# Half of the low parts of x from GpSimd at the change of token halves, and two query columns' attention one step later

## The chip, the cores and the metric

The kernel runs on one core of a Trainium2 chip. The metric is the device time of one execution in microseconds (us); lower is better. The time before is the median of 3 runs.

## The reference, cut to what matters

The reference is one decoder layer: 2048 tokens of width D = 2048 through a normalisation, a sliding-window attention with 32 query heads and 4 key and value heads of 64, a gate, and an output product.

```python
h = rms_norm(x, swa_norm)
q, k, v, gate = split(h @ w_in, [2048, 2048 + 256, 2048 + 512])
q, k = rms_norm(q per head, q_gain), rms_norm(k per head, k_gain)
# blocks of 128 queries against their own and the previous block of keys
s = einsum(q, k) * 64 ** -0.5 + rel_table[t5_bucket(dist)]
s = where(in_band & not before the start, s, -inf)
m = maximum(max(s), sink)
p = exp(s - m); p = p / (sum(p) + exp(sink - m))
o = einsum(p, v)
out = x + (o * silu(gate)) @ w_out
```

All of it is float32. The kernel reaches that on TensorE by splitting each operand into a high and a low part (`h` and `l`) and adding three products: high by high, high by low, low by high.

## The kernel before, in words

**The projections.** The first part of the program has 40 steps. A step is one `gemm` (L147, L150, L153): 128 output columns of q, k or v for 1024 tokens, which is half of the sequence. Its 96 matmuls of 128x512 (16 chunks `k` of D, three products, two token quarters) fill two PSUM banks `acc`, called first and second bank here. Steps 0 to 19 make the first half of the tokens (k, v, eight q columns, k, v, eight q columns), steps 20 to 39 the second half in the same order. Four `acc` buffers serve them, so a step's banks are those of the step two before it, and can start once those have been read out. The weights come as 128x1024 tiles, are split by ACT (`wh`, L132) and POOL (`wl`, L133), with three buffers for each.

**The tokens.** `load_big(c)` brings in x transposed for one half: 16 tiles of 128x1024 through four `raw` buffers; ACT writes the high part scaled by the norm's gain (`bigh`, L100), DVE the low part (`bigl`, L101). For the second half this runs while TensorE works on the last steps of the first half. It is put ahead in priority, once step 19's gemm has been issued.

**The attention.** A `unit` is 256 queries of one query column (two heads): 128 units in all, four per column and half. `beside(n)` issues a step's units from the table `units`. A unit has 8 score matmuls `s` (L328), then on DVE a mask copy, four `lg` (L341), `mx` (L345), `nm` (L347) and `es` (L350), on ACT four exponentials (L354), on DVE `den`, on POOL `lg` times `den` (L359), then 4 transposes `pt` on TensorE (L363), `ph` by ACT (L365), `pl` by DVE (L367), four selects by POOL (L371, L373: `php`, `ph`, `plp`, `pl`), 8 matmuls `o` (L382), `bot` by ACT (L385), two `og` by DVE (L388). The PSUM pools for `s`, `pt` and `o`, and the tiles `ph`, `pl`, `php`, `plp`, have one buffer each, so units follow one another through them hand to hand.

**The hand-over of queries.** `evac_q` reads a q step's two banks: for each bank ACT writes `qq` (L212, in two pieces of 64 rows) and DVE its low part (L213), ACT the squares `sq` (L216). `qq` has four buffers, which is two steps, so the second bank of a step can be read only when the score matmuls that use the buffer from two query steps before have been done; the second bank of the step two later waits for that in its turn. `evac_k` and `evac_v` transpose a k or v step's result on TensorE, normalise and write it out (`kl`, L277).

**The order.** Each engine's instruction order is fixed when the program is built, by a scheduler which follows the program's order and priorities and its own idea of times. So a changed table of units gives another order of TensorE's work, also in places far from the change. Score matmuls of later units, `pt` and `o` of earlier ones, and the projection matmuls of one or two steps stand mixed in TensorE's row. After the 40 steps come gates and the output product (L497 and on), which the change does not touch.

Of the kernel before, what the change touches and what calls it, by code (L numbers as in the profile page):

```python
# [9 lines left out]
F32 = mybir.dt.float32  # L10
F32R = mybir.dt.float32r
I8 = mybir.dt.int8
AF = mybir.ActivationFunctionType
ALU = mybir.AluOpType
# [5 lines left out]
KT = D // P  # L20
HALF = 1024
NB = HALF // P
# [9 lines left out]
def swa_layer_kernel(ctx: ExitStack, tc: tile.TileContext, xT: bass.AP, x: bass.AP, w_in: bass.AP,  # L32
# [13 lines left out]
    nc = tc.nc  # L46
# [36 lines left out]
    gT = const.tile([P, KT], F32, name="gT")  # L83
# [8 lines left out]
    def load_big(c, ks=range(KT), cuts=(0, HALF), xsq=None):  # L92
        hi, lo = [], []
        for k in ks:
            raw = st.tile([P, HALF], F32, tag="raw", name="raw", bufs=RAW)
            h = big.tile([P, HALF], F32R, tag="big", name="bigh")
            l = big.tile([P, HALF], F32R, tag="big", name="bigl")
            for a, b in zip(cuts, cuts[1:]):
                nc.sync.dma_start(out=raw[:, a:b], in_=xT[k * P:(k + 1) * P, c * HALF + a:c * HALF + b])
                nc.scalar.activation(out=h[:, a:b], in_=raw[:, a:b], func=AF.Copy, scale=gT[:, k:k + 1])  # L100
                nc.vector.scalar_tensor_tensor(out=l[:, a:b], in0=raw[:, a:b], scalar=gT[:, k:k + 1],  # L101
                                               in1=h[:, a:b].bitcast(F32), op0=ALU.mult, op1=ALU.subtract)
                if xsq:
                    square_sums(k, raw, a, b, xsq)
            hi.append(h)
            lo.append(l)
        return hi, lo
# [50 lines left out]
    def square_sums(k, raw, a, b, xsq):  # L158

        for i in range(a, b, CH):  # L160
            cs = slice(i, i + CH)
            if k == 0:
                nc.scalar.activation(out=xsq[i // CH], in_=raw[:, cs], func=AF.Square)
            else:
                sq = evp.tile([P, CH], F32, tag="ev", name="xq")
                nc.scalar.activation(out=sq, in_=raw[:, cs], func=AF.Square)
                nc.gpsimd.tensor_tensor(out=xsq[i // CH], in0=xsq[i // CH], in1=sq, op=ALU.add)
# [235 lines left out]
    units = {}  # L403
    for n, (kind, c, i) in enumerate(steps):
        if kind == "q":
            for b in range(0, NB, 2):
                units.setdefault(n + 1 + b // 4, []).append((i, c * NB + b))

    def evacuate(step, acc, copies=None):
        kind, c, i = step  # L410
# [27 lines left out]
    def load_x(k):  # L438
        if k == 0:
            nc.sync.dma_start(out=gT, in_=g_norm)  # L440
        h, l = load_big(0, [k], (0, HALF) if k else (0, CH, HALF), xsq)
        res[0].extend(h)
        res[1].extend(l)
# [25 lines left out]
    for n, step in enumerate(steps):  # L469
        if n < 2:  # L470
            continue
        nxt = load_stat(stat_src(steps[n + 1]), eng=nc.gpsimd) if n + 1 < len(steps) else None
        if 4 <= n < 4 + NB:
            block_sums(NB + n - 4)
        elif n == 4 + NB:
            stats(1)
        beside(n)
        acc = gemm(stat, res)
        if n + 1 < len(steps) and steps[n + 1][1] != step[1]:
            with tc.high_priority(offset=300):  # L480
                res = load_big(1)
        evacuate(step, acc)
        stat = nxt
# [161 lines left out]
    for p, i in tiles:  # L645
# [12 lines left out]
        raw = a  # L658
# [70 lines left out]
```

## Time and profile before

| | us |
|---|---|
| median of 3 runs | 2556.72 (2553.59, 2556.72, 2557.89) |
| the profiled execution, its own time | 2552.12 |
| its span in the profile | 2550.4 |
| TensorE busy | 2467.7 (97%) |
| VectorE busy | 1651.6 (65%) |
| ScalarE busy | 973.7 (38%) |
| GpSimd busy | 1033.5 (41%) |

The granted clock of TensorE over the span was 0.986 of full speed. The busy times are sums over the span; an engine that is busy for two thirds of the whole can be the one that is waited for in a stretch of 30 us. "PE" is TensorE, "DVE" VectorE, "ACT" ScalarE, "POOL" GpSimd. A row of a timeline gives the start of an instruction, its duration, and in brackets the idle time in front of it with the operation that ended the idle time.

### The profile page before, as it was taken

To read this page: it belongs to the slowest core of one execution; us is meant where nothing else is said; L and a number is where in the kernel's file an instruction comes from. 1 tells how busy PE (TensorE), PEld (TensorE's weight loads), DVE (VectorE), ACT (ScalarE), POOL (GpSimd) and SP (SyncE) were. 2 spreads that over 40 slices of the span, in tenths; PEclk is the share of its full clock that TensorE was granted. 3 is DMA by queue.
4 is the path that set the end of the run, shared out by engine and by line. 5 is a ranking of instruction groups with operands and counts; after the bars stand their busy time and mean duration, and the time that the engine had idled before them with its cause. 6 is when DMAs were issued, how large, how long until landed. Compare 5 with 4: busy or idle time off the path is not lost.

```text
span 2550.4 us, 35219 instructions
## 1 busy us (share of the span) xinstructions
PE 2467.7 (97%) x11858; PEld 2048.9 (80%) x11858; DVE 1651.6 (65%) x3220; ACT 973.7 (38%) x2387; POOL 1033.5 (41%) x1011
## 2 busy tenths in 40 slices
PE   7999999999999999999999999999999999998898
PEld 5888888887888888888877887877787877787677
DVE  7387876789788785778737865676764345552432
ACT  6265654456555554455532331332223121121100
POOL 8366665666666675566512300122220220022122
PEclk9999999999999999999999999999999999999999
DMA  5433342125321214122259986887878586676653
GB/s 194 128 106 96 100 130 81 53 83 177 112 73 53 91 57 131 57 70 64 85 195 305 345 290 229 260 279 242 272 255 270 190 286 218 232 261 201 220 176 132
DMA packets 210228, 433.58 MB, mean 170 GB/s; under 512 B 20080, under 2 KB 91392, under 8 KB 210048
## 3 DMA queue, kind: packets, MB, share of 16 engines
q1 hardware_dynamic: 210048, 431.34, 52.2%
q8 instruction: 94, 1.54, 0.2%
q14 instruction: 86, 0.70, 0.1%
HBM read 341.07 MB, written 90.19 MB: 169 GB/s over the span
## 4 chain that ended last, share of the span: by engine, by line
PE 61%; DMA 19%; DVE 10%; issue 6%; POOL 2%; ACT 2%; SPq 1%; DVEq 0%; POOLq 0%; ACTq 0%
PE acc L147 17%; PE acc L153 17%; PE acc L150 17%; PE o L382 4%; PE s L328 4%; DMA braw<-w_out 3%; DMA braw<-xT 3%; DMA araw<-w_in 3%; DMA araw<-o_sp 3%; DMA out<-craw 2%; PE pt L363 2%; DMA araw<-s_sp 2%; DVE araw L497 1%; DVE wl L133 1%; DMA t_sp<-braw 1%
## 5 line engine op out<-in xcount | busy, mean ns | idle before, releaser
L147 PE MATMUL acc<-obh,wh 128*128 128x512 f32 x1536 | 495.8, 398 | 43.2 <-DVE craw L497 20.7
L147 PE MATMUL acc<-bigh,wh 128*128 128x512 f32 x1536 | 506.4, 398 | 15.9 <-ACT bigh L100 8.8
L150 PE MATMUL acc<-bigl,wh 128*128 128x512 f32 x1536 | 500.2, 397 | 3.7 <-DVE bigl L101 3.6
L153 PE MATMUL acc<-bigh,wl 128*128 128x512 f32 x1536 | 497.1, 395 | 1.8 <-DVE wl L133 1.8
L153 PE MATMUL acc<-obh,wl 128*128 128x512 f32 x1536 | 484.3, 394 | 3.6 <-DVE wl L133 3.6
L150 PE MATMUL acc<-obl,wh 128*128 128x512 f32 x1536 | 484.2, 394 | 0.0
L147 PEld LDWEIGHTS acc<-obh,wh 128*128 128x128 f32 x1536 | 293.0, 191 | 123.9 <-issue 19.0
L147 PEld LDWEIGHTS acc<-bigh,wh 128*128 128x128 f32 x1536 | 287.1, 190 | 75.5 <-ACT bigh L100 10.5
L153 PEld LDWEIGHTS acc<-obh,wl 128*128 128x128 f32 x1536 | 291.7, 190 | 67.3 <-DVE wl L133 5.7
L150 PEld LDWEIGHTS acc<-obl,wh 128*128 128x128 f32 x1536 | 292.8, 191 | 60.6
L150 PEld LDWEIGHTS acc<-bigl,wh 128*128 128x128 f32 x1536 | 285.7, 190 | 58.7 <-DVE bigl L101 7.8
L153 PEld LDWEIGHTS acc<-bigh,wl 128*128 128x128 f32 x1536 | 286.3, 189 | 56.6 <-DVE wl L133 2.6
L132 ACT CAST wh<-araw 128x512 fp32r<-128x512 f32 x224 | 137.2, 618 | 454.1 <-PE acc L150 387.9
L500 POOL TENSOR_TENSOR craw<-craw,u 128x512 f32<-128x512 f32 x64 | 89.3, 1406 | 464.4 <-DMA craw<-x 296.0
L354 ACT ACTIVATE lg<-lg,nm 128x128 f32<-128x128 f32 x512 | 199.9, 392 | 193.3 <-DVE nm L347 185.0
L500 POOL TENSOR_TENSOR craw<-craw,th 128x512 f32<-128x512 f32 x64 | 99.0, 1565 | 424.7 <-DVE th L613 353.1
L133 POOL TENSOR_TENSOR wl<-raw,wh 128x512 fp32r<-128x512 f32 x148 | 194.1, 1312 | 107.3 <-ACT wh L132 95.9
L497 DVE TENSOR_TENSOR araw<-araw 128x1024 f32<-128x1024 f32 x64 | 80.9, 1265 | 235.5 <-DMA araw<-o_sp 89.7
L133 DVE TENSOR_TENSOR wl<-araw,wh 128x512 fp32r<-128x512 f32 x224 | 182.3, 821 | 54.4 <-ACT wh L132 49.2
L540 ACT CAST obh<-braw 128x1024 fp32r<-128x1024 f32 x80 | 84.1, 1052 | 256.8 <-DVE braw L497 101.3
L359 POOL TENSOR_TENSOR lg<-lg,den 128x512 f32<-128x512 f32 x128 | 135.9, 1062 | 108.2 <-DVE den L358 68.4
L341 DVE SCALAR_TENSOR_TENSOR lg<-s,rq,bias 128x128 f32<-128x128 f32 x512 | 144.9, 343 | 38.1 <-PE pt L363 22.9
(115 smaller groups left out, 3491.7 us busy)
## 6 DMA issues: line engine op xcount, KB each, us to landing
araw<-w_in SPq DMA_DIRECT2D x88, 512.0 KB, 5.8
braw<-w_out SPq DMA_DIRECT2D x88, 512.0 KB, 5.5
araw<-o_sp SPq DMA_DIRECT2D x88, 512.0 KB, 5.3
raw<-w_in SPq DMA_DIRECT2D x79, 512.0 KB, 3.7
braw<-xT SPq DMA_DIRECT2D x72, 512.0 KB, 5.6
o_sp<-og SPq DMA_DIRECT2D x128, 128.0 KB, 1.9
craw<-o_sp SPq DMA_DIRECT2D x64, 256.0 KB, 4.7
o_sp<-craw SPq DMA_DIRECT2D x64, 256.0 KB, 5.5
```

Source lines behind the costliest of these rows:

```text
L132: nc.scalar.copy(out=h[:, a:b], in_=r)
L133: eng.tensor_tensor(out=l[:, a:b], in0=r, in1=h[:, a:b].bitcast(F32), op=ALU.subtract)
L147: nc.tensor.matmul(acc[n], h[:, cs], res[0][k][:, n * CH:(n + 1) * CH], start=(k == 0), stop=False)
L150: nc.tensor.matmul(acc[n], h[:, cs], res[1][k][:, n * CH:(n + 1) * CH], start=False, stop=False)
L153: nc.tensor.matmul(acc[n], l[:, cs], res[0][k][:, n * CH:(n + 1) * CH], start=False, stop=(k == last))
L328: nc.tensor.matmul(s[:, b, h, lo:], qq[:, h, (i0 + b) * P:(i0 + b + 1) * P], kk[:, i, (i0 + b) * P + lo:(i0 + b + 2) * P], start=(i == 0), ...
L341: nc.vector.scalar_tensor_tensor(out=lg[:, b, h], in0=s[:, b, h, P:], scalar=r, in1=bt[:, h, :], op0=ALU.mult, op1=ALU.add)
L354: nc.scalar.activation(out=lg[:, b, h], in_=lg[:, b, h], func=AF.Exp, bias=nm[:, b, h:h + 1], accum_out=den[:, b, h:h + 1])
L359: nc.gpsimd.tensor_tensor(out=lf, in0=lf, in1=den.rearrange("p b h -> p (b h)").unsqueeze(2).broadcast_to([P, 4, P]), op=ALU.mult)
L382: nc.tensor.matmul(o[:, 2 * b:2 * b + 2, :], v, p[:, 2 * b:2 * b + 2, :], start=(i == 0), stop=(i == len(terms) - 1))
L497: nc.vector.tensor_tensor(out=out, in0=a, in1=b, op=op)
L500: nc.gpsimd.tensor_tensor(out=out, in0=a, in1=b, op=op)
```

## The change

There are two edits. In `load_big`, in the second half and for odd `k`, ACT scales `raw` in place (L101 of the changed kernel), ACT copies it to the high part (L102), and POOL subtracts for the low part (L103); before, one ACT instruction and one DVE instruction did this. Eight of the 16 tiles are concerned. In the table of units, the units of query columns 14 and 15 of the first half are issued one step later.

```diff
--- before.py
+++ after.py
@@ -97,6 +97,11 @@
             l = big.tile([P, HALF], F32R, tag="big", name="bigl")
             for a, b in zip(cuts, cuts[1:]):
                 nc.sync.dma_start(out=raw[:, a:b], in_=xT[k * P:(k + 1) * P, c * HALF + a:c * HALF + b])
+                if c and k % 2:
+                    nc.scalar.activation(out=raw, in_=raw, func=AF.Copy, scale=gT[:, k:k + 1])
+                    nc.scalar.copy(out=h, in_=raw)
+                    nc.gpsimd.tensor_tensor(out=l, in0=raw, in1=h.bitcast(F32), op=ALU.subtract)
+                    continue
                 nc.scalar.activation(out=h[:, a:b], in_=raw[:, a:b], func=AF.Copy, scale=gT[:, k:k + 1])
                 nc.vector.scalar_tensor_tensor(out=l[:, a:b], in0=raw[:, a:b], scalar=gT[:, k:k + 1],
                                                in1=h[:, a:b].bitcast(F32), op0=ALU.mult, op1=ALU.subtract)
@@ -404,7 +409,9 @@
     for n, (kind, c, i) in enumerate(steps):
         if kind == "q":
             for b in range(0, NB, 2):
-                units.setdefault(n + 1 + b // 4, []).append((i, c * NB + b))
+
+                later = int(c == 0 and i >= KT - 2)
+                units.setdefault(n + 1 + b // 4 + later, []).append((i, c * NB + b))
 
     def evacuate(step, acc, copies=None):
         kind, c, i = step
```

In the changed kernel the lines behind the first edit have numbers higher by 5, those behind the second by 7. TensorE's row is the same in both kernels for the first 2884 instructions; from there to the end of the attention it is ordered anew. Three places of it follow. In the names, `acc` is a bank of a gemm, and the number behind a name tells buffers' generations apart.

TensorE at the second bank of step 21. In the order before, what stands between the last score matmul of unit 55 (column 13, the fourth unit) and the first matmul of that bank:

```order
L328 MATMUL s_6871<-kk_6412,qq_6368 128x256
L363 MATMUL pt_6841<-ident_150,lg_6821 128x128 x4
L382 MATMUL o_6642<-php_6636,vv_6136 128x256
L382 MATMUL o_6642<-plp_6639,vv_6136 128x256
L382 MATMUL o_6642<-ph_6632,vv_6136 128x256
L328 MATMUL s_6933<-kk_6135,qq_6757 128x128 x4
L328 MATMUL s_6933<-kk_6135,qq_6757 128x256 x4
...
L382 MATMUL o_6642<-pl_6634,vv_6136 128x256
L147 MATMUL acc_7840<-bigh_7151,wh_7284 128x512
```

And in the order of the change, between the same two:

```order
L333 MATMUL s_6871<-kk_6412,qq_6368 128x256 x8
...
L387 MATMUL o_6521<-pl_6513,vv_6413 128x256
L152 MATMUL acc_7727<-bigh_7082,wh_7181 128x512
L155 MATMUL acc_7727<-bigl_7083,wh_7181 128x512
...
L158 MATMUL acc_7727<-bigh_7101,wl_7182 128x512
L368 MATMUL pt_6627<-ident_150,lg_6607 128x128 x4
L152 MATMUL acc_7728<-bigh_7030,wh_7171 128x512
```

Before, 4 transposes, 8 `o` and 8 `s` stand there and no projection matmul; now 5 `o`, 12 projection matmuls of the first bank and 4 transposes.

TensorE at steps 30 and 31, from the score matmuls of unit 87 (column 5 of the second half, its last unit). In the order before, both banks of step 30 run beside it:

```order
L328 MATMUL s_10483<-kk_10023,qq_9979 128x256 x8
L363 MATMUL pt_10239<-ident_150,lg_10219 128x128 x4
L150 MATMUL acc_11061<-bigl_7182,wh_10409 128x512
L150 MATMUL acc_11062<-bigl_7182,wh_10409 128x512
L382 MATMUL o_10194<-php_10188,vv_9746 128x256
L382 MATMUL o_10194<-plp_10191,vv_9746 128x256
L382 MATMUL o_10194<-ph_10184,vv_9746 128x256
L153 MATMUL acc_11061<-bigh_7181,wl_10410 128x512
```

In the order of the change the last matmul of step 31's first bank stands ahead of it, and the second bank behind two more rounds of units:

```order
L158 MATMUL acc_11365<-bigh_7101,wl_10820 128x512
L333 MATMUL s_10491<-kk_10031,qq_9987 128x256 x8
L368 MATMUL pt_10247<-ident_150,lg_10227 128x128 x4
L387 MATMUL o_10202<-php_10196,vv_9754 128x256
...
L333 MATMUL s_10553<-kk_9753,qq_10377 128x256 x8
L368 MATMUL pt_10461<-ident_150,lg_10441 128x128 x4
L387 MATMUL o_10262<-php_10256,vv_9754 128x256
...
L333 MATMUL s_10613<-kk_9753,qq_10377 128x256 x8
L152 MATMUL acc_11366<-bigh_7030,wh_10809 128x512
```

So 48 instructions (three times 8 `s`, twice 4 transposes, twice 8 `o`) now stand in a row with no projection matmul among them.

TensorE at the end of the attention, behind the last projection matmul. Before:

```order
L153 MATMUL acc_15045<-bigh_7193,wl_15041 128x512
L363 MATMUL pt_14765<-ident_150,lg_14745 128x128 x4
L382 MATMUL o_14720<-php_14714,vv_13542 128x256
...
L382 MATMUL o_14780<-php_14774,vv_13542 128x256
...
L147 MATMUL acc_15127<-bigh_7151,wh_15119 128x512
```

In the order of the change:

```order
L158 MATMUL acc_15053<-bigh_7075,wl_15049 128x512
L368 MATMUL pt_14713<-ident_150,lg_14693 128x128 x4
L387 MATMUL o_14536<-php_14530,vv_13272 128x256
...
L368 MATMUL pt_14773<-ident_150,lg_14753 128x128 x4
L387 MATMUL o_14728<-php_14722,vv_13550 128x256
...
L387 MATMUL o_14788<-php_14782,vv_13550 128x256
...
L152 MATMUL acc_15135<-bigh_7030,wh_15127 128x512
```

Each `o` row stands for 8 matmuls of one unit: two units' worth before, three now.

## Rows read from the trace of the kernel before

**Rows 1.** The page, part 1: busy us of each engine, share of the span, count.

```profile
PE 2467.7 (97%) x11858; PEld 2048.9 (80%) x11858; DVE 1651.6 (65%) x3220; ACT 973.7 (38%) x2387; POOL 1033.5 (41%) x1011
```

**Rows 2.** Windows of core 0: sum, then busy us of PE, PEld, DVE, ACT, POOL; clock, DMA.

```profile
555.00:620.00 65.00, 62.67 (x322) 50.64 (x320) 60.29 (x121) 43.02 (x96) 36.83 (x35) 1.00 0.54 172
620.00:650.00 30.00, 26.74 (x123) 21.89 (x124) 26.50 (x73) 16.62 (x54) 17.87 (x24) 0.83 0.21 71
650.00:680.00 30.00, 27.62 (x164) 24.03 (x163) 19.68 (x50) 14.11 (x43) 21.44 (x22) 1.00 0.40 107
680.00:1280.00 600.00, 600.00 (x3290) 517.50 (x3289) 463.90 (x1207) 306.43 (x941) 372.78 (x421) 1.00 0.25 79
1280.00:1310.00 30.00, 26.08 (x124) 21.57 (x123) 11.86 (x27) 10.29 (x29) 10.33 (x14) 0.89 0.29 100
```

**Rows 3.** Timeline of PE, steady stretch: start us, us, engine line op.

```profile
1260.39 0.62 PE L147 MATMUL acc<-bigh,wh 128*128 128x512 f32 x2
1260.84 0.62 PE L150 MATMUL acc<-bigl,wh 128*128 128x512 f32 x2
...
1263.57 0.60 PE L363 MATMUL pt<-ident,lg 128*128 128x128 f32 x4
1263.92 0.71 PE L150 MATMUL acc<-bigl,wh 128*128 128x512 f32 x2
1264.47 0.28 PE L382 MATMUL o<-php,vv 128*128 128x256 f32 x1
...
1265.41 1.11 PE L328 MATMUL s<-kk,qq 128*128 128x256 f32 x8
1266.36 0.64 PE L153 MATMUL acc<-bigh,wl 128*128 128x512 f32 x2
```

**Rows 4.** Timeline of PE ahead of step 21's second bank.

```profile
634.92 0.28 PE L328 MATMUL s<-kk,qq 128*128 128x256 f32 x1
636.67 0.63 PE L363 MATMUL pt<-ident,lg 128*128 128x128 f32 x4 [1.47 <-DVE pl L367]
637.95 0.55 PE L382 MATMUL o<-php,vv 128*128 128x256 f32 x1 [0.64 <-POOL plp L371]
...
642.43 0.80 PE L147 MATMUL acc<-bigh,wh 128*128 128x512 f32 x1 [0.73 <-ACT sq L216]
...
647.72 0.47 PE L147 MATMUL acc<-bigh,wh 128*128 128x512 f32 x1
```

**Rows 5.** Timeline of ACT in the same stretch.

```profile
636.28 0.58 ACT L212 CAST qq<-acc 64x512 fp32r<-64x512 f32 x1
...
641.78 0.60 ACT L216 ACTIVATE sq<-acc 128x512 f32<-128x512 f32 x1
```

**Rows 6.** The same stretch on DVE.

```profile
638.47 0.69 DVE L213 TENSOR_TENSOR qq<-acc,qq 64x512 fp32r<-64x512 f32 x1
```

**Rows 7.** Timeline of PE at the key step's evacuation behind the change of halves.

```profile
667.77 0.63 PE L363 MATMUL pt<-ident,lg 128*128 128x128 f32 x4 [1.47 <-DVE pl L367]
669.30 0.47 PE L147 MATMUL acc<-bigh,wh 128*128 128x512 f32 x1 [0.91 <-DVE kl L277]
```

**Rows 8.** Timeline of PE at the end of the attention.

```profile
1298.57 0.36 PE L382 MATMUL o<-php,vv 128*128 128x256 f32 x1 [2.24 <-DVE og L388]
...
1302.54 0.79 PE L147 MATMUL acc<-bigh,wh 128*128 128x512 f32 x1 [1.33 <-ACT u L683]
```

**Rows 9.** Groups by line and form, 540 to 1300 us: busy us, mean ns of one.

```profile
L133 POOL TENSOR_TENSOR wl<-raw,wh 128x512 fp32r<-128x512 f32 x85 | 112.6, 1325 | 42.4 <-ACT wh L132 32.5 <-PE acc L153 8.2 <-ACT qq L212 1.2
...
L101 DVE SCALAR_TENSOR_TENSOR bigl<-raw,gT,bigh 128x1024 fp32r<-128x1024 f32 x16 | 21.6, 1354 | 3.1 <-ACT bigh L100 3.0
L100 ACT ACTIVATE bigh<-raw,gT 128x1024 fp32r<-128x1024 f32 x16 | 18.4, 1150 | 14.1 <-DMA raw<-xT 13.3 <-PE acc L150 0.7
```

**Rows 10.** The page, part 5: a copy of a 128x1024 tile by ACT.

```profile
L540 ACT CAST obh<-braw 128x1024 fp32r<-128x1024 f32 x80 | 84.1, 1052 | 256.8 <-DVE braw L497 101.3
```

**Rows 11.** The instructions of line L347: shortest, median, longest ns.

```profile
L347 DVE SCALAR_TENSOR_TENSOR nm<-mx,nsink x128: 134/164/1307, 125.3 to 1286.3; 128x4 f32<-128x4 f32 x128
```

## The prediction

> **What bounds the kernel now.** I read the busy times first, then the windows, then the timeline of TensorE where a window shows a loss. TensorE is busy 97% of the span [rows 1], so only its gaps and its slow stretches can be won or added. The windows say where these lie [rows 2]: between 680 and 1280 us TensorE is busy 600.00 of 600.00 us, so the attention of the second half costs nothing but TensorE's own work, and any wait that the change puts there is a pure loss. Ahead of it stand the losses that the change is aimed at: 65.00 - 62.67 = 2.33 us at 555 to 620, where the second half's x is loaded; 30.00 - 26.74 = 3.26 us at 620 to 650, and there the granted clock is 0.83, which is 26.74 x 0.17 = 4.5 us more; 2.38 us at 650 to 680. At the end of the attention, 1280 to 1310, are 3.92 us idle, and the clock is 0.89.
>
> The unit costs at full clock are from a steady stretch [rows 3], from start to start: a projection matmul 0.45 / 2 = 0.225 us, four transposes 0.35, eight `o` 0.94, eight `s` 0.95.
>
> The 620 to 650 loss is one pile [rows 4]. The last score matmul of unit 55 ends at 635.2; the second bank of step 21 starts at 642.43, 7.2 us later, though only 0.35 + 0.94 + 0.95 = 2.25 us of work stands between. So 4.95 us are lost, in waits for `pl`, `plp` and at last `sq`. Then the matmuls run at half clock (1.2 GHz) until 647.72: the twelve from 642.43 on take 5.29 us, where twelve cost 2.7 at full clock: 2.6 us more. The pile costs 7.5 us, which agrees with the window's 7.8. It is the hand-over of queries: once the scores are done, `qq` is cast, its low part made, the second piece cast, the squares taken. Bare that is 0.58 + 0.69 + 0.58 + 0.60 = 2.5 us [rows 5, 6]; it took 7.2, since other units' work stands between on both queues (the cast begins at 636.28, the squares at 641.78).
>
> **The change part by part.**
>
> The order of TensorE in the changed kernel (above) is not the old one with units moved, so I cost its three places rather than the idea.
>
> (a) Low parts on GpSimd. DVE loses 8 x 1.354 = 10.8 us and POOL gains eight subtractions of 128x1024; a 128x512 one takes 1.325 us [rows 9], so two of those each, 21.2 us. ACT keeps the scaling (1.150 us, rows 9) and gains a copy: 8 x 1.052 = 8.4 us [rows 10]. In the 65 us of the load phase that makes DVE 49.5, ACT 51.4 and POOL 58.0 us of work [rows 2]. The fullest queue goes from DVE's 93% to POOL's 89%: the pressure moves to the engine that also makes `wl` and every unit's four selects. Behind each 2.65 us subtraction such work queues, and `raw` is held longer, until POOL has read it, so its next load starts later. Bounds: 0 (all of it beside TensorE's work) and 8 x 1.325 = 10.6 us (each subtraction delays TensorE by half its length). I take 2.3 us, the loss that the stretch shows under a queue as full as that.
>
> (b) The pile at step 21. Now 5 `o`, 12 projection matmuls and 4 transposes stand between unit 55's scores and the bank: 0.6 + 2.7 + 0.35 = 3.65 us of work. The hand-over takes between 2.5 (bare) and 7.2 us; I take 4, nearer the bare one, since DVE has less queued. So 0.35 us stay lost, and -7.5 + 0.35 = **-7.2 us**. Bounds: -7.8 (the whole window) and 7.2 - 3.65 = 3.55 still lost with the clock low, -1.4.
>
> (c) The key step behind it. Its evacuation costs 1.47 + 0.91 = 2.4 us before [rows 7], where transposes that wait for `pl` stand ahead of the bank. In the new order no transposes of a unit stand there; half of it goes: -1.2 us, between -2.4 and 0.
>
> (d) Steps 30 and 31. The later units make a new pile: three sets of scores, two of transposes and two of `o` in a row with no projection matmul, 5.4 us of work, where before both banks of step 30 ran beside this and nothing was lost [rows 2]. The same kinds of hand-over as in the pile of step 21 stand there, two rounds of them. I take that pile's idle time, +5.0 us. Bounds: one wait of the kind in [rows 7], 2.4; and that pile and another round's wait of 2.24 [rows 8], 7.2. The clock fell in the pile of step 21 and at the end of the attention, and did not at the waits of [rows 7], where the window has 1.00 [rows 2]. The new pile lies between, being busy 5.4 us of about 10.4: I take half of 4.5, +2.2, between 0 and 4.5. Then the key step 30 is evacuated in the sequence of [rows 7], which before was spread over projection matmuls: +2.4, between 0 and 2.4.
>
> (e) The end of the attention. TensorE has one more round of `o` (eight matmuls, and the transposes ahead of them) behind the last projection matmul. A round that nothing covers waited 2.24 us [rows 8]: +2.5 us with its transposes, between 1 and 4.
>
> Sum: 2.3 - 7.2 - 1.2 + 5.0 + 2.2 + 2.4 + 2.5 = **+6.0 us**. The profiled execution would go from 2552.1 to 2558.1. It lies 4.6 us below the median of the runs, so on the median of 2556.7 the sum gives **2562.7 us**. About 0.2%, 5.1 us, is what a measurement of this kernel can tell from no change.
>
> **The rivals.**
>
> *The pile is gone and none takes its place* (the other side). At step 31 no load of x runs beside the units: DVE has 463.90 of 600 us of work there (77%) and ACT 306.43 (51%), against DVE's 26.50 of 30 (88%) at the old pile [rows 2]. If the queues are empty enough, the hand-overs run at their bare 2.5 us, the 5.4 us of unit work cover them, and terms (d) come to about 0. It decides whether `pl` and the selects come before TensorE needs them. Then -7.2 - 1.2 + 2.5 with (a) at 0: -5.9, 2550.8 us. Against it: rounds of units with nothing between lost time at both places where the trace has them [rows 4, 8].
>
> *It cancels.* The new pile costs one wait only, the clock stays up, (a) is hidden: -7.2 - 1.2 + 2.4 + 2.4 + 2.5 = -1.1, 2555.6 us.
>
> *POOL holds DVE.* A DVE operation on 128x4, `nm`, takes 164 ns as a rule and once up to 1307 [rows 11], which is about the length of a POOL subtraction [rows 9]. If each of the eight longer ones holds one such operation for 1.325 us on the path, (a) is 10.6 rather than 2.3: 2562.7 + 8.3 = 2571.0 us. For it: `nm` stands ahead of the exponentials of every unit. Against it: DVE has 10.8 us less to do in that stretch, so that a held operation can be made good there.
> The Trainium skill, "SBUF — State Buffer", section "Who interferes with whom", has the rule: a DVE instruction with two SBUF inputs contends with a GpSimd instruction that reads SBUF, and the one that comes second is blocked until the first ends. The longest `nm` agrees with it; it speaks against a longer subtraction on GpSimd. By the rule the removed DVE subtraction was itself such a two-input instruction, so some blocking goes with it.
>
> *The change does less than it says.* The table moves eight units by a step, but the scheduler orders freely, and DVE's work waits for POOL's: if the hand-over at step 21 still takes 7.2 us, (b) is -1.4 and the sum +11.8, 2568.5 us. I count it within the main case's range.
>
> **How the numbers follow.** Main case, a moved pile: 0.40, of 2557 to 2570, its centre hardly above the 0.2%, so 0.28 of it slower and 0.12 the same. POOL holds DVE: 0.14, slower. It cancels: 0.21, the same. No new pile: 0.25, faster. So faster 0.25, same 0.33, slower 0.42. The likeliest case gives 2562.7 us. The range that leaves out a tenth on each side reaches down past the faster case's 2550.8 to 2549 and up to 2572, just past POOL's case.
>
> **What would show it.** Right: at 620 to 650 us the clock is 1.00 and no gap before step 21's second bank is over 1 us; near 950 to 1000 us a gap of TensorE of several us with `s`, `pt` and `o` around it, and the clock below 1 behind it; three rounds of `o` before the gate's first matmul. Wrong: 680 to 1280 stays at 600.00 busy (then it is faster), or the load phase alone loses over 5 us, with `nm` and `den` longer than a microsecond while L103 runs (then POOL's case).

## The result, and the profile after

The changed kernel takes **2567.45 us** (median of 7 runs), the kernel before 2555.95 us in the same comparison (7 runs): ratio 1.0053, 95% interval 1.0037 to 1.0069. It is 11.5 us slower. The prediction was slower by 6.0 us, 2562.7 us, with a range of 2549 to 2572.

The windows of the changed kernel, with the columns of [rows 2]:

```profile
555.00:620.00 65.00, 60.04 (x304) 49.12 (x303) 54.72 (x119) 47.88 (x102) 51.45 (x41) 0.97 0.49 159
620.00:650.00 30.00, 28.65 (x154) 24.04 (x153) 25.22 (x60) 19.39 (x50) 21.61 (x20) 1.00 0.38 129
650.00:680.00 30.00, 29.41 (x163) 25.18 (x162) 20.59 (x48) 13.59 (x38) 21.76 (x26) 1.00 0.47 131
680.00:940.00 260.00, 259.50 (x1411) 222.72 (x1410) 193.66 (x509) 129.03 (x399) 160.18 (x182) 1.00 0.23 71
940.00:960.00 20.00, 17.74 (x93) 14.93 (x94) 19.45 (x55) 11.62 (x34) 13.11 (x15) 0.91 0.08 23
960.00:980.00 20.00, 16.63 (x87) 14.12 (x86) 12.40 (x30) 9.03 (x35) 13.34 (x14) 0.91 0.46 126
...
1280.00:1310.00 30.00, 27.66 (x155) 23.23 (x153) 17.53 (x45) 12.51 (x40) 13.70 (x20) 1.00 0.17 53
1310.00:1340.00 30.00, 26.82 (x104) 21.66 (x105) 9.19 (x12) 8.42 (x14) 2.49 (x4) 0.83 0.70 235
```

Against [rows 2]: the old pile at 620 to 650 is gone (28.65 busy, clock 1.00, where 26.74 and 0.83 stood), 650 to 680 lost 0.6 us rather than 2.4. The load phase lost 2.6 us more and a little clock. At 940 to 980, where TensorE had no idle time before, 5.6 us are idle and the clock is 0.91. TensorE's timeline shows both halves of that, the units' rounds at 943 to 949 and the key step's evacuation at 971:

```profile
943.02 0.63 PE L368 MATMUL pt<-ident,lg 128*128 128x128 f32 x4 [0.91 <-POOL lg L364]
944.37 0.36 PE L387 MATMUL o<-php,vv 128*128 128x256 f32 x1 [0.72 <-DVE og L393]
...
946.70 2.05 PE L333 MATMUL s<-kk,qq 128*128 128x256 f32 x8 [0.24 <-DVE es L355]
948.55 0.63 PE L152 MATMUL acc<-bigh,wh 128*128 128x512 f32 x1
...
971.49 0.63 PE L368 MATMUL pt<-ident,lg 128*128 128x128 f32 x4 [2.43 <-DVE pl L372]
973.05 0.58 PE L387 MATMUL o<-php,vv 128*128 128x256 f32 x1 [0.93 <-POOL php L376]
973.43 0.63 PE L152 MATMUL acc<-bigh,wh 128*128 128x512 f32 x1
```

The matmul at 948.55 is the first of step 31's second bank, the one at 973.43 follows the key step's `kn` transposes. And the end of the attention, which has three rounds of `o` where [rows 8] has two:

```profile
1306.80 0.63 PE L368 MATMUL pt<-ident,lg 128*128 128x128 f32 x4 [1.49 <-DVE pl L372]
...
1311.86 0.55 PE L387 MATMUL o<-php,vv 128*128 128x256 f32 x1 [2.24 <-DVE og L393]
1315.83 0.80 PE L152 MATMUL acc<-bigh,wh 128*128 128x512 f32 x1 [1.32 <-ACT u L690]
```

The gate's first matmul comes at 1315.83 rather than 1302.54 [rows 8], 13.3 us later; 2.4 of these were there at 550 us already, ahead of anything that the change moves, so the change's part is 10.9. What follows took 2562.8 - 1315.8 = 1247.0 us, and 2550.4 - 1302.5 = 1247.9 before. So the loss lies ahead of the gate, all of it.

### The profile page after: what moved, and what is told of

Same layout as the page of the kernel before. It is cut to its first block, busy times and chain, and to the rows that moved or that the text cites. A ratio compares the mean times of both kernels' runs of the same rounds, so it can differ in the third digit from the quotient of the medians.

```text
span 2562.8 us, 35236 instructions
## 1 busy us (share of the span) xinstructions
PE 2465.2 (96%) x11858; PEld 2044.6 (80%) x11858; DVE 1647.4 (64%) x3212; ACT 981.6 (38%) x2395; POOL 1048.6 (41%) x1019
## 4 chain that ended last, share of the span: by engine, by line
PE 57%; DMA 20%; DVE 12%; issue 5%; ACT 3%; POOL 2%; SPq 1%; DVEq 0%; ACTq 0%; POOLq 0%
PE acc L152 16%; PE acc L155 16%; PE acc L158 16%; DMA braw<-w_out 5%; DMA braw<-xT 4%; PE o L387 4%; PE s L333 4%; DMA araw<-s_sp 2%; DMA araw<-o_sp 2%; DMA araw<-w_in 2%; PE pt L368 2%; DMA out<-craw 2%; DVE wl L138 1%; DVE braw L504 1%; DMA t_sp<-braw 1%
## 5 line engine op out<-in xcount | busy, mean ns | idle before, releaser
L155 PE MATMUL acc<-bigl,wh 128*128 128x512 f32 x1536 | 506.1, 397 | 4.9 <-DVE bigl L106 2.7
L158 PE MATMUL acc<-bigh,wl 128*128 128x512 f32 x1536 | 504.6, 396 | 1.7 <-DVE wl L138 1.4
```

Source lines behind the costliest of these rows:

```text
L155: nc.tensor.matmul(acc[n], h[:, cs], res[1][k][:, n * CH:(n + 1) * CH], start=False, stop=False)
L158: nc.tensor.matmul(acc[n], l[:, cs], res[0][k][:, n * CH:(n + 1) * CH], start=False, stop=(k == last))
```

## The experiments

Two theories stood at the start. **A**: the order of TensorE's work decides; the old pile goes because projection matmuls stand in the hand-over of queries, and a new one comes at step 31 because none do. **B**: GpSimd's eight longer subtractions are the loss, since they hold DVE and delay units. All diffs are against the changed kernel, unless said otherwise.

**The first edit alone.**

```diff
-                later = int(c == 0 and i >= KT - 2)
+                later = 0
```

> Only the first edit: the eight odd low parts on POOL, all units at their old steps. In its order 12 projection matmuls stand between unit 55's scores and step 21's second bank (as in the change), no pile ahead of step 31's second bank, and ten projection matmuls ahead of the last round of o. Theory A (the loss of the change is the moved pile, made by the later units; the first edit alone removes the old pile): load phase +4.4, pile at step 21 -6.4, key step -1.8, 680 to 1280 within 1 us of 600 busy, end of the attention -2 to 0: 4 to 6 us faster than before, ratio 0.997 to 1.000. Rival B (the subtractions on POOL are the loss: they hold DVE and delay every unit): as slow as the change, ratio 1.003 to 1.006, and 940 to 980 shows the same gaps.

Measured: 2544.29 us against 2550.83, ratio 0.9971 (0.9960 to 0.9982): faster by 6.5 us.

```profile
555.00:620.00 65.00, 59.54 (x303) 48.76 (x302) 54.48 (x118) 48.46 (x102) 51.93 (x41) 0.97 0.48 159
620.00:650.00 30.00, 28.93 (x155) 24.17 (x154) 24.44 (x60) 17.35 (x48) 22.11 (x21) 1.00 0.31 107
...
940.00:980.00 40.00, 40.00 (x234) 35.25 (x234) 31.66 (x80) 22.73 (x73) 27.25 (x34) 1.00 0.47 131
```

The load phase and the step 21 window are those of the change, and 940 to 980 is full. So all eight subtractions on GpSimd do not by themselves make the loss: B falls. The pages of this run and of the change count the same instructions on every engine (DVE 3212, ACT 2395, GpSimd 1019), so that these two kernels differ in their order alone, and by the two ratios 0.8% in time.

**The second edit alone.** The kernel before with the table of the change: the five lines of the first edit taken out.

> Only the second edit: units of columns 14 and 15 one step later, all low parts on DVE. In its order no projection matmul stands between unit 55's scores and step 21's second bank, only 3.3 us of unit work; more than 20 projection matmuls stand ahead of step 31's second bank. Theory A as refined by the order (a gap comes only where unit work stands without projection matmuls in the hand-over of queries): the pile at step 21 stays, 4 to 6 us idle and a low clock behind it, no gap at 940 to 980, so the same as before, ratio 0.998 to 1.002. If the later units by themselves were what removes the old pile and makes the new one: clock 1.00 at 620 to 650 and gaps at 940 to 980.

Measured: 2539.42 us, ratio 0.9951 (0.9937 to 0.9966). Faster, where "the same" was expected.

```profile
620.00:650.00 30.00, 26.23 (x148) 21.96 (x148) 27.49 (x69) 16.31 (x53) 20.36 (x25) 1.00 0.22 73
650.00:680.00 30.00, 28.89 (x163) 24.73 (x162) 21.96 (x61) 16.82 (x51) 22.48 (x23) 1.00 0.51 141
...
940.00:980.00 40.00, 40.00 (x234) 34.73 (x232) 31.61 (x80) 23.07 (x76) 27.56 (x34) 1.00 0.52 144
```

The pile at step 21 is there as expected (3.77 us idle at 620 to 650, more than before's 3.26), and 940 to 980 is full. But the clock stayed at 1.00, where a low one was expected. TensorE's timeline in it:

```profile
633.74 0.60 PE L363 MATMUL pt<-ident,lg 128*128 128x128 f32 x4
...
636.90 1.16 PE L328 MATMUL s<-kk,qq 128*128 128x128 f32 x8 [1.85 <-DVE lg L341]
...
640.23 0.50 PE L147 MATMUL acc<-bigh,wh 128*128 128x512 f32 x1
640.57 0.40 PE L150 MATMUL acc<-bigl,wh 128*128 128x512 f32 x1
```

From the scores' end to the bank it is 640.23 - 633.74 = 6.5 us with 3.3 us of work, and the matmuls behind run at 0.23 us from start to start, where twelve took 0.44 in [rows 4]. The gate's first matmul comes at 1298.3, 4.2 us earlier than before. The rest of its gain lies behind the attention, where the span's last part took 2532.9 - 1298.3 = 1234.6 us, 13.3 less than before; more on that below.

So each edit alone is faster, and both together are slower. Neither "the subtractions" nor "the later units" carries the loss.

**Four tiles instead of eight, with and without later units.**

```diff
-                if c and k % 2:
+                if c and k % 4 == 3:
```

> Both edits, but only every fourth low part on POOL (k = 3, 7, 11, 15: four subtractions rather than eight). In its order 14 projection matmuls stand in the hand-over at step 21 and 24 at step 31; the end is that of before. Theory A: neither pile is there, the load phase costs half of the change's 4.4: -6.4 - 1.8 + 2 = 6 us faster than before, ratio 0.997 to 0.999. Rival B: half of the change's loss, ratio 1.002 to 1.003.

The second of the two has `later = 0` as well.

> Four low parts on POOL (k = 3, 7, 11, 15) and all units at their old steps. In its order 14 projection matmuls stand in the hand-over at step 21 and 27 at step 31. Theory A: as the run with both edits and four subtractions, ratio 0.997 to 0.999, so that the later units add nothing. Rival B: ratio 1.002 to 1.003. If the later units are needed: slower than the run that has them by over 2 us.

Measured: 2537.19 us, ratio 0.9944 (0.9929 to 0.9959), and 2541.91 us, ratio 0.9960 (0.9945 to 0.9974). Both have clock 1.00 at 620 to 650 and 40.00 of 40 busy at 940 to 980. A's sign holds, but both gain more than it said, and most of that is not A's: it lies behind the attention (table below). The second is 4.7 us slower than the first, which was to be the sign that the later units are needed; that difference, too, lies behind the attention, 1240.8 against 1233.8 us. A's size of the load phase does not hold: with half of the subtractions it loses as much as with all, with later units

```profile
555.00:620.00 65.00, 60.12 (x304) 49.76 (x304) 55.91 (x118) 42.22 (x96) 42.57 (x36) 0.97 0.47 156
```

and at their old steps even more, 58.88 busy.

**The subtraction by DVE, from the scaled tile.** With `later = 0`, and

```diff
-                    nc.gpsimd.tensor_tensor(out=l, in0=raw, in1=h.bitcast(F32), op=ALU.subtract)
+                    nc.vector.tensor_tensor(out=l, in0=raw, in1=h.bitcast(F32), op=ALU.subtract)
```

> The first edit without its GpSimd part: ACT scales odd tiles in place and copies them to the high part, but DVE makes the low part as before; units at their old steps. In its order 20 or more projection matmuls stand in the hand-over at steps 21 and 31. If GpSimd's queue makes the load phase slower (60.04 of 65 busy and clock 0.97 in the change, against 62.67 and 1.00): load phase as before, no pile at 620 to 650, no gap at 940 to 980: ratio 0.994 to 0.997. If ACT's second pass over the tile makes it: 555 to 620 as in the change, ratio 0.996 to 0.999.

Measured: 2545.82 us against 2555.90, ratio 0.9964 (0.9947 to 0.9980), no gap at 940 to 980, and

```profile
555.00:620.00 65.00, 59.68 (x304) 49.21 (x302) 59.00 (x126) 48.01 (x103) 39.95 (x35) 0.97 0.50 161
620.00:650.00 30.00, 28.71 (x163) 24.48 (x162) 27.47 (x70) 19.61 (x58) 20.97 (x20) 1.00 0.28 93
```

GpSimd is back at 40 of 65 us, and the load phase loses 5.3 us, the change 5.0, with the same clock. So GpSimd's eight subtractions are not needed for its loss. Other waits stand in their place, most of them for the units' own work on GpSimd:

```profile
608.31 0.66 PE L368 MATMUL pt<-ident,lg 128*128 128x128 f32 x4 [1.45 <-POOL lg L364]
611.12 0.38 PE L387 MATMUL o<-php,vv 128*128 128x256 f32 x1 [1.69 <-POOL php L376]
```

**GpSimd alone, without ACT's second pass.** With `later = 0`, every fourth tile, and

```diff
-                    nc.scalar.activation(out=raw, in_=raw, func=AF.Copy, scale=gT[:, k:k + 1])
-                    nc.scalar.copy(out=h, in_=raw)
+                    nc.scalar.activation(out=h, in_=raw, func=AF.Copy, scale=gT[:, k:k + 1])
+                    nc.gpsimd.tensor_scalar(out=raw, in0=raw, scalar1=gT[:, k:k + 1], scalar2=None, op0=ALU.mult)
```

> Every fourth tile: ACT as in the kernel before (one pass), GpSimd scales the tile in place and subtracts (two instructions of it, four tiles, so as many GpSimd instructions as in the change), no work taken by ACT; units at their old steps. In its order 16 projection matmuls stand in the hand-over at step 21 and 28 at step 31. If ACT's second pass is what makes 555 to 620 lose 5 us and the clock there: 62 or more of 65 busy, clock 1.00. If GpSimd's queue or its hold on DVE: 60 or less, clock 0.97 or lower.

Measured: 2549.87 us against 2551.40, ratio 0.9992 (0.9978 to 1.0006).

```profile
555.00:620.00 65.00, 57.87 (x270) 47.77 (x270) 55.88 (x112) 38.31 (x88) 48.75 (x37) 0.89 0.43 136
```

ACT is no fuller than before (38.31 us) and the load phase loses more than ever. So ACT's second pass is not needed for the loss either. By their expectations the fifth run points at ACT's pass and this one at GpSimd; neither fits both runs. The longest waits are different ones again, 2.95 us for ACT's `sq` and 2.46 for DVE's `lg`.

Of the ten kernels, the two that keep the pile at step 21 (before, and the later units alone) have 61.7 to 62.7 us busy in the load phase, the other eight 57.9 to 60.1. What the eight share is a changed load of x and, with it, another order of TensorE's work there; the later units alone keep the order of before up to 624 us. No run has the one without the other, so the cause of this loss stays open.

**The second half's columns 6 and 7 later too.** This keeps the change's order ahead of step 31's second bank, word for word, and restores the end to two rounds.

```diff
-                later = int(c == 0 and i >= KT - 2)
+                later = int(c == 0 and i >= KT - 2 or c == 1 and i in (6, 7))
```

> The change, and the units of columns 6 and 7 of the second half one step later as well. TensorE's order ahead of step 31's second bank is word for word that of the change (48 instructions without a projection matmul); the end is that of before (two rounds of o). If the order is what costs: the same gaps of about 5 us and the low clock at 940 to 980, and the third round's 2 to 3 us at the end gone: 2 to 5 us under the change, still slower than before, ratio 1.001 to 1.005. If the later units of the first half by themselves are the cause and not the order behind it, no reading of the order would tell, and the time is that of the change or above.

Measured: 2556.27 us against 2555.90, ratio 1.0008 (0.9992 to 1.0024): by the two ratios 11 us under the change, where 2 to 5 were expected.

```profile
940.00:980.00 40.00, 38.33 (x209) 32.86 (x210) 29.47 (x86) 23.04 (x73) 28.64 (x33) 0.96 0.41 119
...
1280.00:1310.00 30.00, 26.44 (x128) 21.93 (x127) 12.68 (x35) 11.51 (x32) 10.01 (x16) 0.89 0.27 91
```

```profile
940.20 0.63 PE L368 MATMUL pt<-ident,lg 128*128 128x128 f32 x4 [0.91 <-POOL lg L364]
941.55 0.35 PE L387 MATMUL o<-php,vv 128*128 128x256 f32 x1 [0.72 <-DVE og L393]
```

TensorE's row is that of the change up to step 31's second bank (953 us in the change), and the same rows give the same gaps, 0.91 and 0.72 us. The wait of the key step (2.43 and 0.93 in the change) is not there: behind its `kn` transposes stand projection matmuls now.

```profile
962.15 1.03 PE L251 MATMUL acc<-ident,kn 128*128 128x128 f32 x8
962.94 0.71 PE L158 MATMUL acc<-bigh,wl 128*128 128x512 f32 x2
```

So the loss at 940 to 980 has two parts that can come apart, the pile and the key step behind it: 3.9 and 4.9 us in the profile of the change, 4.0 and 2.9 in its repeat below.

**Both kernels once more.**

> The kernel before, once more, for how much two profiles of one program differ: the start of the gate's first matmul (1302.5 us) within 3 us, the stretch behind it (1247.9 us) within 4 us if a program's order decides it, up to 13 us apart if it varies from run to run.

> The changed kernel, once more: the gate's first matmul at 1315.8 within 3 us, with the same gaps ahead of step 31's second bank, and the stretch behind it 1247.0 us within 4.

Measured, one run each: 2552.51 and 2562.82 us; the gate's first matmul at 1302.44 and at 1312.75 us, the second 3.1 us off where 3 were allowed; the last parts 2550.8 - 1302.4 = 1248.4 and 2561.11 - 1312.75 = 1248.4 us. The gaps repeat to a hundredth in many rows (0.91, 0.72, 0.20; at the end 1.49 and 2.24), the clock does not: 940 to 980 had 0.96 this time, 34.77 busy.

**The change with DVE in GpSimd's place.** Both edits, with the diff of the fifth run and the change's own table: in the program's text only the engine of eight subtractions differs from the change.

> Both edits, but DVE makes the odd low parts from the scaled tile, not GpSimd: of the change only the engine of eight subtractions is undone. In its order 20 or more projection matmuls stand in the hand-overs of queries at steps 21 and 31, and there is no third round of o at the end. If the order of TensorE decides: no gap at 940 to 980, no pile at 620 to 650, load phase as in the run with the scaled low part on DVE alone (59.7 busy, clock 0.97), the gate's first matmul near 1296. Behind it SP's queue stands as in the two runs whose last part took 1234 us (later units alone; a quarter of the low parts): if that order decides the last part, the span is 1296 + 1234 = 2530, ratio 0.990 to 0.994; if those two were chance, the span is 1296 + 1248 = 2544, ratio 0.995 to 0.998. If the later units are what loses time in the change, whatever the engine: ratio 1.002 to 1.005.

Measured: **2532.95 us** against 2551.40, ratio 0.9925 (0.9905 to 0.9944), 18 us faster than before. It is the lowest ratio here, though its interval overlaps that of four tiles with later units.

```profile
555.00:620.00 65.00, 59.59 (x304) 49.17 (x303) 59.26 (x128) 47.07 (x102) 39.58 (x36) 0.97 0.49 163
620.00:650.00 30.00, 28.91 (x159) 24.50 (x158) 28.37 (x68) 19.38 (x50) 21.07 (x21) 1.00 0.29 97
650.00:680.00 30.00, 30.00 (x172) 26.13 (x171) 20.84 (x55) 16.85 (x56) 20.48 (x24) 1.00 0.60 167
...
940.00:980.00 40.00, 40.00 (x234) 35.04 (x233) 27.00 (x73) 21.29 (x70) 27.28 (x33) 1.00 0.53 148
...
1280.00:1310.00 30.00, 27.83 (x129) 22.76 (x128) 8.92 (x16) 9.96 (x23) 6.57 (x9) 0.94 0.46 153
```

```profile
1294.67 0.39 PE L387 MATMUL o<-pl,vv 128*128 128x256 f32 x1 [0.74 <-POOL pl L378]
1296.86 0.50 PE L152 MATMUL acc<-bigh,wh 128*128 128x512 f32 x1 [1.32 <-ACT u L690]
```

No pile at step 21, none at step 31, no third round. The gate's first matmul comes at 1296.86 (1296 was expected) and the last part takes 2532.1 - 1296.9 = 1235.2 us (1234). The later units are in it, so they are not by themselves what loses time; the order that the scheduler makes of both edits with GpSimd is.

Two stretches of each profile tell where the times come from. The first runs from the eight `s` that start at 573.09 us in before to the gate's first matmul; up to those `s`, TensorE's row is the same in all kernels. The second is what follows, to the end of the span.

| kernel | ratio | to the gate, us | behind it, us |
|---|---|---|---|
| before, twice | 1 | 729.4, 731.5 | 1247.9, 1248.4 |
| the change, twice | 1.0053 | 740.4, 738.5 | 1247.0, 1248.4 |
| first edit alone | 0.9971 | 723.5 | 1247.3 |
| later units alone | 0.9951 | 724.7 | 1234.6 |
| four tiles, later units | 0.9944 | 727.3 | 1233.8 |
| four tiles | 0.9960 | 728.1 | 1240.8 |
| scaled low part by DVE | 0.9964 | 723.0 | 1254.3 |
| GpSimd alone | 0.9992 | 730.1 | 1239.3 |
| later units in both halves | 1.0008 | 730.4 | 1252.0 |
| the change with DVE | 0.9925 | 722.2 | 1235.2 |

Ahead of the gate, too, each edit alone is below before and both together above it. Four tiles gain no more there than the two profiles of before differ by, and the larger part of the gain of the three kernels with 1234 to 1235 us lies behind.

## Why the prediction was right, and where its steps were off

The sign, the range and the likeliest case held: a pile that moved. The size, +6.0 us, is about half of the 11.5 measured. The terms by [rows 2] and the windows after, idle time and clock together:

| term | predicted | measured | how |
|---|---|---|---|
| (a) load phase | +2.3 | +4.4 | idle 2.33 to 4.96, and 60 x 0.03 of clock |
| (b) pile at step 21 | -7.2 | -6.4 | 7.8 to 1.35 |
| (c) key step behind it | -1.2 | -1.8 | 2.38 to 0.59 |
| (d) steps 30 and 31 | +9.6 | +8.7 | 5.63 idle at 940 to 980, and 34.4 x 0.09 of clock |
| (e) the end | +2.5 | +3.3 | 6.8 to 10.1 at 1280 to 1340, idle and clock (before lost nothing at 1310 to 1340) |

The sum is 8.2 us against 6.0 predicted; single gaps elsewhere in 680 to 1280, 0.5 + 0.8 us, bring it to 9.5. The 10.9 us at the gate's first matmul and the 11.5 of the medians lie above that by 1.4 and 2.0, within what the profile's clock column, rounded to a hundredth, leaves open; and the second profiles of both kernels differ ahead of the gate by 7.0 us rather than 10.9, so that no term is known to better than some 2 us.

**(b)** was right by its own step. The hand-over was put at 4 us with 3.65 us of work beside it. It took 4.6: unit 55's scores end at 636.3, the second bank starts at 640.85, and TensorE is busy nearly all the time.

```profile
635.34 1.10 PE L333 MATMUL s<-kk,qq 128*128 128x256 f32 x8
...
640.85 0.50 PE L152 MATMUL acc<-bigh,wh 128*128 128x512 f32 x1
```

That projection matmuls in the hand-over are what removes the pile is shown by contrast: all eight kernels that have ten or more of them there have 27.7 to 29.4 of 30 us busy and clock 1.00; the later units alone, with none, has 26.23.

**(d)** was wrong in its split, and right in its sum by luck, since two errors nearly cancel in this profile. The pile was put at 5.0 + 2.2 us, the key step at 2.4. The gaps of the pile are 2.3 us by 960, and 17.7 x 0.09 = 1.6 of clock, 3.9 in all; the key step's are 3.4 and 1.5 of clock, 4.9. The step that failed is "I take that pile's idle time, +5.0 us". Of the old pile's 4.95 us only 1.47 + 0.64 + 0.73 = 2.84 are waits [rows 4]. Most of the rest is unit work at half clock, as in this row of before,

```profile
638.73 1.91 PE L328 MATMUL s<-kk,qq 128*128 128x128 f32 x8
```

where the same eight `s` take 1.16 us at full clock (later units alone, at 636.90); and half clock was added once more with the 2.2. The 48 instructions at step 31 wait 0.91 + 0.72 + 0.24 us in the rows shown and 0.74 in four short ones, 2.6 in all, about as long as the old pile did. The rival of the emptier queues did not come true: DVE was busy 19.45 of 20 us at 940 to 960. The key step was sized too small for this profile: its waits are 2.43 + 0.93 rather than 1.47 + 0.91, and its clock had no term. In the repeat they are 1.92 + 0.93 and the clock stayed up, 2.9 us in all; the pile's 3.9 are 4.0 there. So it is the pile's size that was firmly wrong.

**(a)** was sized too small, and its reason is not borne out. 1.8 us of the 4.4 are clock, for which it had no term. The step "the pressure moves to the engine that also makes `wl` and every unit's four selects" does not explain the loss: without the eight subtractions (fifth and last run above) it is as large. That it lay between the bounds was luck. In the change itself one of the subtractions is behind the longest gap, 2.08 of the 5.0 us idle:

```profile
614.61 1.22 PE L155 MATMUL acc<-bigl,wh 128*128 128x512 f32 x2 [2.08 <-POOL bigl L103]
```

```profile
609.97 2.28 POOL L138 TENSOR_TENSOR wl<-raw,wh 128x512 fp32r<-128x512 f32 x1
612.22 2.34 POOL L103 TENSOR_TENSOR bigl<-raw,bigh 128x1024 fp32r<-128x1024 f32 x1
```

```profile
611.01 1.26 DVE L352 SCALAR_TENSOR_TENSOR nm<-mx,nsink 128x4 f32<-128x4 f32 x1
612.31 2.27 DVE L355 TENSOR_TENSOR es<-nm,sink 128x4 f32<-128x4 f32 x1
```

`nm` ends at 612.27, when GpSimd's `wl` ends (612.25), and `es` at 614.58, when `bigl` does (614.56): two operations on 128x4, of which `nm` takes 0.16 us as a rule [rows 11], took 3.5 together. That is the mechanism of the rival "POOL holds DVE", seen here as described, and it agrees with the Trainium skill, "SBUF — State Buffer", section "Who interferes with whom": of a DVE instruction with two SBUF inputs and a GpSimd instruction that reads SBUF, the second waits for the first. The sign named for this rival came in part: the load phase has 4.96 us idle, 5.49 in the repeat, and `es` and later a `den` of 1.35 us end with a `bigl` of GpSimd. But of `nm`, `es` and `den` only three were longer than a microsecond at 540 to 625 us, where before has two of 1.25 us; the rival counted on eight. It did not decide the time: the first edit alone has all eight subtractions and is 6.5 us faster than before.

**The cause as the prediction told it** was too simple in one point. It put (b) to the change as a whole and said "the later units make a new pile". By the runs, the later units alone make none at step 31, and the first edit alone removes the old pile. The new one is a product of both in this one order: with DVE as the engine, the same table gives no pile at all.

The repeat of the change shows how firm the sizes are: the load phase had 59.51 busy, 940 to 980 34.77 with clock 0.96 rather than 0.91. The idle time repeats within half a microsecond, the clock's part by two.

## What to carry to other kernels

Where a scheduler orders the program, an edit's price is the price of the order that comes out, and that has to be read at every hand-over, not at the edited place alone: count what stands between the last reader of a buffer and the first writer that waits for it. Here a dozen projection matmuls between the last scores and the next bank were enough; where none stood, the pile cost 4 to 8 us, the key step behind it not counted. Two edits that each gain can lose together, so each is run alone before either is judged.

## What was not expected of the hardware and the program

**The clock does not follow the idle time of a stretch.** At 620 to 650 us, 3.26 us idle went with clock 0.83 [rows 2], and 3.77 us with 1.00 in the run of the later units alone. In the slow case unit work itself was at half clock in the pile and the twelve projection matmuls behind it; in the other case there were gaps of 1.85 us ahead of the bank and 0.98 at 647.86, and unit work at full clock around them. The change and its repeat differ in the same way, 0.91 and 0.96 at 940 to 980 with nearly the same idle time. What makes the difference isn't settled.

**The part behind the attention has its own order and its own time.** It took 1234 to 1254 us (table above). The three with 1233.8 to 1235.2 us have one order there, of DMA issues and on every engine. That it would be fast again was on record before the change with DVE ran. Some 7 us lie in one place: before waits there for a product of DVE,

```profile
1530.55 0.50 PE L147 MATMUL acc<-obh,wh 128*128 128x512 f32 x1 [0.78 <-DVE w L497]
1543.99 1.00 PE L147 MATMUL acc<-obh,wh 128*128 128x512 f32 x2 [2.51 <-DVE w L497]
```

and the 512 matmuls around it take 124 us in before against 116 in those three. The order does not fix the whole: before (twice), the scaled low part by DVE and GpSimd alone share one order behind the gate as well, take 122 to 124 us at that place, and 1239 to 1254 us in all. The medians speak for the order even so. Less the 1.7 us by which a run's own time exceeds its span, and less the profile's time of the gate, those of one comparison leave 1247.1 us for before, 1247.3 for GpSimd alone and 1234.4 for the change with DVE (an estimate: it takes the gate's time to be that of the profile in every run). Why the order does this was not tried.
